# Gate and up multiplied together in a float32 decoder layer, two of eight chunk pairs by Strassen's seven products

## The chip, the cores and the metric

The kernel runs on one core of a Trainium2 chip. The metric is the device time of one execution in microseconds (us); lower is better. TensorE (PE) multiplies and transposes, VectorE (DVE) and ScalarE (ACT) work elementwise, GpSimd (POOL) does a few sums and issues DMAs, and SyncE (SP) issues most of the DMAs.

## The reference

A decoder layer on 256 tokens of width 2048, all in float32: a SwiGLU feed-forward, a mixer (attention and RWKV-7), cross-attention into a memory, a second feed-forward and a final norm. The change touches the two feed-forwards, the first loads and the last norm with its stores.

```python
D_MODEL = 2048
...
SEQ = 256
...
D_FF = 5632
...
def rms_norm(x, g):
    xf = x.astype(jnp.float32)
    y = xf * lax.rsqrt(jnp.mean(xf * xf, axis=-1, keepdims=True) + NORM_EPS)
    return (y * g.astype(jnp.float32)).astype(x.dtype)

def swiglu(h, w_gate, w_up, w_down):
    return (jax.nn.silu(h @ w_gate) * (h @ w_up)) @ w_down
...
        x = x + 0.5 * swiglu(rms_norm(x, ffn1_norm[l]), ffn1_w_gate[l], ffn1_w_up[l], ffn1_w_down[l])
...
        x = x + 0.5 * swiglu(rms_norm(x, ffn2_norm[l]), ffn2_w_gate[l], ffn2_w_up[l], ffn2_w_down[l])
    return rms_norm(x, final_norm)
```

## The kernel before

**Products.** A float32 factor is kept as two parts, hi (rounded to the type float32r) and lo (what is left). One float32 product is three TensorE products that accumulate in PSUM: hi by hi, hi by lo, lo by hi (`multiply`, lines 336 to 338). The stationary operand is a 128x128 piece of the activations: 128 features of one chunk k, 128 tokens; the two halves of the 256 tokens are t = 0 and 1. The moving operand is 128 features by 512 columns of a weight, and the result is a PSUM bank of 128 tokens by 512 columns.

**Weights.** They come from HBM once, in the order of `plan`. A unit is two chunks (KU = 2, called a chunk pair here) by 512 columns. `load` issues its DMA on SP's queue; in the feed-forwards one load fetches two units, 1 MB, into one of four buffers `raw2` (elsewhere one unit into one of four buffers `raw`). `divide` splits a unit: ScalarE casts raw to hi (line 299), VectorE subtracts to get lo (line 300). There are three buffers of each, so a unit can be split when the third unit before it has been multiplied. `next_unit` loads up to eight units ahead and splits up to two ahead (AHEAD). A unit serves 12 products: two chunks, two token halves, three parts.

**A feed-forward.** `feed_forward` goes through eleven blocks j of 512 columns of the hidden layer, in groups of 4, 4 and 3. A block is two calls of `product`, each over eight units (KD = 16 chunks): gate, whose two banks ScalarE turns into silu (line 415), then up, whose two banks VectorE multiplies by the row scale r and the silu (line 418) into `hb`. The result is then transposed on TensorE in two steps of four and split into hi and lo (`transposed`, lines 347, 352 and 353); these steps are interleaved with the products of what follows. After a group come four products with the down weights.

**Order.** The program is written as one stream; `bg` (class Interleave) holds generators of side work, and each `bg.tick()` between products lets every group of them take a step. A scheduler then places each engine's instructions, and every engine runs its own queue in that fixed order, waiting on semaphores.

**PSUM** has eight banks: three `acc` for products, three `mm` for the mixer, two `tr` for transposes.

**Opening and end.** Line 239 fills the first norm's gain by way of TensorE. SP first loads the sinks, then x in two halves of its first 512 columns with 1 MB of gate weights after each (lines 456 to 461). In the second feed-forward POOL's queue reloads x and loads the final gain early (`reload`); at the end line 1183 stores each half of the tokens in four DMAs on SP's queue.

Of the kernel before, what the change touches and what calls it, by code (L numbers as in the profile page):

```python
# [15 lines left out]
P = 128  # L16
# [20 lines left out]
EDGES = (34, 71)  # L37
# [42 lines left out]
def feed_forward_plan(wg, wu, wd):  # L80
    for j0, nj in GROUPS:
        for j in range(j0, j0 + nj):
            for w in (wg, wu):
                yield w, 0, KD, j * 512, 512
        for n in range(4):
            yield wd, 4 * j0, 4 * nj, n * 512, 512


def weight_plan(a):

    w = {n: v[0] for n, v in a.items() if "_w_" in n or n.startswith("w_")}
    yield from feed_forward_plan(w["ffn1_w_gate"], w["ffn1_w_up"], w["ffn1_w_down"])
    w_in = w["w_in"]
# [21 lines left out]
    for n in range(4):  # L115
        yield w["w_cross_o"], 0, 4, n * 512, 512
    yield from feed_forward_plan(w["ffn2_w_gate"], w["ffn2_w_up"], w["ffn2_w_down"])
# [3 lines left out]
def decoder_layer(ctx: ExitStack, tc: tile.TileContext, a: dict, out: bass.AP):  # L121
# [41 lines left out]

    def select(out, in_, pattern, op, fill, base, mult):
# [40 lines left out]
    nc.sync.dma_start(sinks[:], a["attn_sinks"].broadcast_to([P, 16]))  # L205
# [62 lines left out]
    plan = list(weight_plan(a))  # L268
    units = [(w, k0 + k, c0, n) for w, k0, nk, c0, n in plan for k in range(0, nk, KU)]
    raws, parts = {}, {}  # L270
    at = {"unit": 0, "product": 0, "pool": None}
    ends = [sum(nk // KU for _, _, nk, _, _ in plan[:i]) for i in (EDGES[0], EDGES[1])]

    def load(u):
# [10 lines left out]
        for i in range(m):  # L285
            raws[u + i] = raw[:, i * KU : (i + 1) * KU, :]
        nc.sync.dma_start(
            raw[:], w[k * P : (k + m * KU) * P, c0 : c0 + n].rearrange("(a p) n -> p a n", p=P)
        )

    def divide(u):
        if u >= len(units) or u in parts:
            return
# [3 lines left out]
        for s in (slice(0, 1), slice(1, 2)) if u == 0 else (slice(0, KU),):  # L297
# [3 lines left out]
        parts[u] = hi, lo  # L301

    def next_unit():
        u = at["unit"]
        at["unit"] += 1
        for v in range(u, u + (2 * LOADED if at["pool"] is not None else LOADED)):
            load(v)
            if v <= u + AHEAD:
                divide(v)
        return parts[u]  # L310

    def product(x: Act, w, skew=False):
# [6 lines left out]
        for k in range(0, nk - KU * len(skewed), KU):  # L319
            bg.until(lambda: all(k + i in x.done for i in range(KU)))  # L320
            u = next_unit()
# [3 lines left out]
        last = [(k, next_unit()) for k in skewed]  # L325
# [4 lines left out]

    def multiply(o, x, u, k, t, nk):
        hi, lo = u
        s = slice(t * P, (t + 1) * P)
        for i in range(KU):
            xh, xl = (x.at(p, k + i)[:, s] for p in range(2))
            pe.matmul(o, xh, hi[:, i, :], start=k + i == 0, stop=False)  # L336
            pe.matmul(o, xh, lo[:, i, :], start=False, stop=False)  # L337
            pe.matmul(o, xl, hi[:, i, :], start=False, stop=k + i == nk - 1)  # L338
# [60 lines left out]
    def feed_forward(sp, x, norm: Norm, wg, wu, wd, done, last=False):  # L399
        for gi, (j0, nj) in enumerate(GROUPS):  # L400
# [10 lines left out]
            for j in range(j0, j0 + nj):  # L411
                pg = product(norm.x, wg)
                hb = sp.tile([P, 2, 512], F32, tag="hb", name="hb", bufs=3)
# [7 lines left out]
                bg.spawn("feat", transposed(hb, 4 * (j - j0)))  # L421
            for n in range(4):
# [24 lines left out]
    with tc.tile_pool(name="f1", bufs=1, reuse_waits="tile") as sp:  # L447
# [695 lines left out]
    with tc.tile_pool(name="f2", bufs=1, reuse_waits="tile") as sp:  # L1143
# [3 lines left out]
        fin = sp.tile([P, D], F32, name="fin")  # L1147

        def reload():
            for n in range(4):  # L1150
# [3 lines left out]
                yield from idle(4)  # L1154
                pool.dma_start(
                    fin[:, cb], a["final_norm"][cb].unsqueeze(0).broadcast_to([P, 512])
                )
# [56 lines left out]
```

## Time and profile before

| | us |
|---|---|
| median of three timed runs | 2323.39 (2322.45 to 2326.1) |
| the profiled execution | 2329.57 |
| its span | 2327.9 |
| TensorE busy in the span | 2303.2 |
| VectorE busy | 1261.3 |
| ScalarE busy | 1078.0 |
| POOL busy | 130.9 |

Durations below are from the one profiled execution. The products of TensorE overlap, so that its busy time counts more than the time a product adds; the distance between starts is the better measure. The DMAs moved 432.71 MB, 185 GB/s over the span counting HBM's side.

### The profile page before, as it was taken

Reading aid. Unit: us, or ns where it says so; the run is one execution under the profiler, and the core shown is the slowest. Engines: PE = TensorE matmul, PEld = TensorE weight load, DVE = VectorE, ACT = ScalarE, POOL = GpSimd, SP = SyncE. Lnnn points to the kernel's source line nnn. Section 1 sums busy time; section 2 is a strip of 40 time slices with the busy share of each in tenths; the row PEclk is TensorE's granted clock in tenths of the full one; section 3 lists DMA queues with packets and bytes.
Section 4 is the critical chain, followed back from the end, with each engine's and each line's share of the span. In section 5 each row is a group of like instructions: output and inputs, shape, how many; then the busy total and the mean of one; then the engine's idle time right before and its main releaser. Section 6 shows DMA issues by size and latency. Waiting matters only on the chain.

```text
span 2327.9 us, 27346 instructions
## 1 busy us (share of the span) xinstructions
PE 2303.2 (99%) x10853; PEld 1893.5 (81%) x10853; DVE 1261.3 (54%) x1395; ACT 1078.0 (46%) x1425; POOL 130.9 (6%) x192
## 2 busy tenths in 40 slices
PE   8999999999999999999999999999999999999998
PEld 7888888888888877778888888888888888888886
DVE  4545544554556467886444466546545544554545
ACT  5443344434445468534434446455444344434444
POOL 1000000000000000200320030001000000000001
PEclk9999999999999999999999999999999999999999
DMA  8565655556554544677533576648555565556653
GB/s 291 182 196 184 198 187 193 186 193 197 183 193 151 170 129 135 198 214 212 151 85 96 158 259 217 201 154 298 192 188 191 190 197 183 197 183 197 192 188 127
DMA packets 219856, 432.71 MB, mean 186 GB/s; under 512 B 14267, under 2 KB 17040, under 8 KB 219728
## 3 DMA queue, kind: packets, MB, share of 16 engines
q1 hardware_dynamic: 211520, 405.58, 54.7%
q0 software_dynamic: 8176, 25.38, 3.4%
q8 instruction: 85, 1.39, 0.2%
q14 instruction: 43, 0.35, 0.0%
q10 hardware_dynamic: 32, 0.01, 0.0%
HBM read 417.56 MB, written 13.11 MB: 185 GB/s over the span
## 4 chain that ended last, share of the span: by engine, by line
PE 92%; issue 4%; DMA 2%; DVE 1%; ACT 1%; POOL 0%; SPq 0%; ACTq 0%; POOLq 0%; DVEq 0%
PE acc L336 28%; PE acc L337 28%; PE acc L338 28%; PE tr L347 2%; PE mm L924 1%; PE tr L893 1%; DVE lo L300 0%; PE mm L542 0%; DMA raw<-in_ffn_w_gate_dram 0%; DMA raw<-in_w_out_dram 0%; ACT hi L299 0%; PE tr L911 0%; DMA raw<-in_w_in_dram 0%; ACT s L567 0%; PE tr L994 0%
## 5 line engine op out<-in xcount | busy, mean ns | idle before, releaser
L300 DVE TENSOR_TENSOR lo<-raw,hi 128x1024 fp32r<-128x1024 f32 (+1 forms) x769 | 943.2, 1227 | 956.0 <-ACT hi L299 955.4
L299 ACT CAST hi<-raw 128x1024 fp32r<-128x1024 f32 (+1 forms) x769 | 805.4, 1048 | 1061.2 <-PE acc L338 1027.8
L336 PE MATMUL acc<-hi,xhi 128*128 128x512 f32 (+1 forms) x2016 | 799.5, 397 | 1.4 <-ACT hi L299 1.2
L337 PE MATMUL acc<-lo,xhi 128*128 128x512 f32 (+1 forms) x2016 | 787.2, 390 | 2.1 <-DVE lo L300 2.1
L338 PE MATMUL acc<-hi,xlo 128*128 128x512 f32 (+1 forms) x2016 | 785.9, 390 | 0.0
L336 PEld LDWEIGHTS acc<-hi,xhi 128*128 128x128 f32 x2016 | 380.3, 189 | 82.9 <-issue 5.4
L337 PEld LDWEIGHTS acc<-lo,xhi 128*128 128x128 f32 x2016 | 380.7, 189 | 81.1 <-DVE lo L300 3.3
L338 PEld LDWEIGHTS acc<-hi,xlo 128*128 128x128 f32 x2016 | 380.2, 189 | 79.2 <-issue 1.0
L336 PE MATMUL acc<-hi,hhi 128*128 128x512 f32 x704 | 275.5, 391 | 0.0
L338 PE MATMUL acc<-hi,hlo 128*128 128x512 f32 x704 | 274.2, 389 | 0.0
L337 PE MATMUL acc<-lo,hhi 128*128 128x512 f32 x704 | 274.0, 389 | 0.0
L338 PEld LDWEIGHTS acc<-hi,hlo 128*128 128x128 f32 x704 | 132.1, 188 | 27.8
L336 PEld LDWEIGHTS acc<-hi,hhi 128*128 128x128 f32 x704 | 132.2, 188 | 26.9
L337 PEld LDWEIGHTS acc<-lo,hhi 128*128 128x128 f32 x704 | 132.2, 188 | 26.9
L336 PE MATMUL acc<-hi,mthi 128*128 128x512 f32 x128 | 51.2, 400 | 0.0
L338 PE MATMUL acc<-hi,mtlo 128*128 128x512 f32 x128 | 50.1, 392 | 0.0
L337 PE MATMUL acc<-lo,mthi 128*128 128x512 f32 x128 | 49.9, 390 | 0.0
L1167 POOL TENSOR_TENSOR x<-x,fin 128x512 f32<-128x512 f32 x6 | 8.9, 1505 | 692.1 <-ACT junk L1165 692.1
L470 POOL DMA_DIRECT2D x1d<-x x4 | 3.0, 744 | 710.4 <-DVE x L427 710.4
L415 ACT ACTIVATE hb<-acc,rs 128x512 f32<-128x512 f32 x44 | 30.2, 690 | 19.5 <-PE acc L338 19.5
L352 ACT CAST hhi<-tr 128x512 fp32r<-128x512 f32 x44 | 25.7, 584 | 16.3 <-PE tr L347 16.3
L373 ACT ACTIVATE xhi<-tr,gains 128x256 fp32r<-128x256 f32 x48 | 22.0, 471 | 22.8 <-DVE xlo L374 16.1
(290 smaller groups left out, 1625.5 us busy)
## 6 DMA issues: line engine op xcount, KB each, us to landing
raw<-in_ffn_w_up_dram SPq DMA_DIRECT2D x88, 1024.0 KB, 5.2
raw<-in_ffn_w_down_dram SPq DMA_DIRECT2D x88, 1024.0 KB, 5.1
raw<-in_ffn_w_gate_dram SPq DMA_DIRECT2D x86, 1024.0 KB, 5.2
raw<-in_w_in_dram SPq DMA_DIRECT2D x136, 512.0 KB, 3.7
raw<-in_w_out_dram SPq DMA_DIRECT2D x32, 512.0 KB, 4.6
raw<-in_w_proj_attn_dram SPq DMA_DIRECT2D x16, 512.0 KB, 3.7
raw<-in_w_proj_rwkv_dram SPq DMA_DIRECT2D x16, 512.0 KB, 5.9
raw<-in_w_cross_kv_dram SPq DMA_DIRECT2D x16, 512.0 KB, 3.6
```

The source lines that it names most:

```text
L299: act.copy(hi[:, s], raw[:, s])
L300: dve.tensor_tensor(lo[:, s], raw[:, s], f32(hi[:, s]), ALU.subtract)
L336: pe.matmul(o, xh, hi[:, i, :], start=k + i == 0, stop=False)
L337: pe.matmul(o, xh, lo[:, i, :], start=False, stop=False)
L338: pe.matmul(o, xl, hi[:, i, :], start=False, stop=k + i == nk - 1)
L347: pe.transpose(b[:, o : o + P], tok[:, t, col : col + P], ident[:])
L352: act.copy(x.at(0, c, n), src)
L373: last = act.activation(self.x.at(0, c), b[:, j, :], AF.Copy, scale=g)
L415: act.activation(hb[:, t, :], pg[t][:], AF.Silu, scale=norm.r[t])
L893: pe.matmul(b[e][:, m * P : (m + 1) * P], x1[r, j, cs_], x2[r, j, cs_], start=True, stop=True,)
L924: pe.matmul(vb[:, o : o + P][:, r], lhs(e), rhs[:, r], start=first and e == 0, stop=True, **ek,)
L1167: pool.tensor_tensor(xs, xs, fin[:, n * 512 : (n + 1) * 512], ALU.mult)
```

## The change

Blocks j = 1 to 10 of each feed-forward multiply gate and up together (`product_pair`); j = 0 and the down products stay as they were. An item is then a unit of gate and the unit of up for the same chunks, and `next_item` loads and splits by items. For the chunk pairs 0, 2, 4, 5, 6 and 7 an item costs four times six products, as before. For pairs 1 and 3 (SEVEN) the two chunks, two token halves and two weights form a 2 by 2 times 2 by 2 product, which is done by Strassen's scheme in Winograd's form: seven products (each of three parts) in place of eight. `sums` makes the four combinations of the weights on VectorE and splits them; `combinations` makes those of the activations on POOL once per feed-forward. The seven products accumulate in seven banks p1 to p7 (three mm, two acc, two tr) over both pairs; after pair 3 VectorE adds p1, p6, p7 and p5 to what the other banks collect (`u2`, `u3`), and pair 0 (EARLY) uses differences of activations for p3, so that the sum comes out. After the last pair VectorE adds these to p2, p4, p3 and p5.

The opening gives TensorE nine products of ones, loads x by 512 columns and the first gate weights in smaller pieces, one of them on ScalarE's queue, and moves the sinks' load to POOL's queue. The final gain is loaded in the last group of the second feed-forward into two `raw` buffers. The last stores are three per half, on SP's and ScalarE's queues. `hb` has two buffers in place of three.

```diff
+SEVEN = (1, 3)
+EARLY = tuple(q for q in range(max(SEVEN)) if q not in SEVEN)
...
+            if j == 0:
+                for w in (wg, wu):
+                    yield w, 0, KD, j * 512, 512
+            else:
+                yield (wg, wu), 0, KD, j * 512, 512
...
+    idle_bank = mm()
+    for _ in range(9):
+        pe.matmul(idle_bank[:, :P], ones[:], ones[:], start=True, stop=True)
...
-    nc.sync.dma_start(sinks[:], a["attn_sinks"].broadcast_to([P, 16]))
+    pool.dma_start(sinks[:], a["attn_sinks"].broadcast_to([P, 16]))
...
+        for k in range(k0, k0 + nk, 2 * KU):
+            u = len(units)
+            units += [(v, k + i, c0, n) for v in w for i in (0, KU)]
+            items += [(u, u + 2), (u + 1, u + 3)]
...
+    def sums(g, u):
...
+        sp, rg, ru = at["pool"], raws[g], raws[u]
+        ta, tb = (wp.tile([P, KU, 512], F32, tag="raw", name="raw", bufs=4) for _ in range(2))
+        hi = sp.tile([P, 4, 512], F32R, tag="thi", name="thi")
+        lo = sp.tile([P, 4, 512], F32R, tag="tlo", name="tlo")
+        dve.tensor_tensor(ta[:, 0], ru[:, 0], rg[:, 0], ALU.subtract)
+        dve.tensor_tensor(ta[:, 1], ru[:, 1], ru[:, 0], ALU.subtract)
+        dve.tensor_tensor(tb[:, 0], ru[:, 1], ta[:, 0], ALU.subtract)
+        dve.tensor_tensor(tb[:, 1], rg[:, 1], tb[:, 0], ALU.subtract)
+        for i, t in enumerate((ta, tb)):
+            act.copy(hi[:, 2 * i : 2 * i + 2], t[:])
+            dve.tensor_tensor(
+                lo[:, 2 * i : 2 * i + 2], t[:], f32(hi[:, 2 * i : 2 * i + 2]), ALU.subtract
+            )
+        return hi, lo
+
+    def divide(i):
...
+        g, u = items[i]
+        if units[g][1] // KU in SEVEN:
+            parts[i] = split_unit(g), split_unit(u, slice(1, 2)), sums(g, u)
+        else:
+            parts[i] = split_unit(g), split_unit(u)
+
+    def next_item():
+        i = at["item"]
+        at["item"] += 1
+        u = items[i][0]
         for v in range(u, u + (2 * LOADED if at["pool"] is not None else LOADED)):
             load(v)
...
+        divide(i)
+        room = AHEAD
+        for j in range(i + 1, min(i + 1 + AHEAD, len(items))):
+            room -= len(items[j])
+            if room < 0:
+                break
+            for v in items[j]:
+                load(v)
+            divide(j)
+        return parts[i]
...
+    def combinations(sp, x: Act):
...
+            for q in range(max(SEVEN) + 1):
+                while not {2 * q, 2 * q + 1} <= x.done:
+                    yield
...
+                pool.tensor_tensor(
+                    v[:].rearrange("p k t n -> p k (t n)"), f32(x.at(0, 2 * q, 2)),
+                    f32(x.at(1, 2 * q, 2)), ALU.add,
+                )
+                if q in SEVEN:
+                    n = 4
+                    pool.tensor_tensor(f[:, 0], v[:, 0, 1], v[:, 1, 1], ALU.add)
+                    pool.tensor_tensor(f[:, 1], f[:, 0], v[:, 0, 0], ALU.subtract)
+                    pool.tensor_tensor(f[:, 2], v[:, 0, 0], v[:, 0, 1], ALU.subtract)
+                    pool.tensor_tensor(f[:, 3], v[:, 1, 0], f[:, 1], ALU.subtract)
+                else:
+                    n = 2
+                    pool.tensor_tensor(f[:, :2], v[:, :, 0], v[:, :, 1], ALU.subtract)
+                yield from idle(3)
+                s = slice(o, o + n)
+                act.copy(parts[0][:, s], f[:, :n])
+                dve.tensor_tensor(parts[1][:, s], f[:, :n], f32(parts[0][:, s]), ALU.subtract)
...
+    def product_pair(sp, x: Act, c, r, w):
...
+        def add(to, x_, w_, last):
+            if to not in b:
+                b[to] = {"p1": mm, "p3": mm, "p5": mm, "p2": acc, "p4": acc}.get(to, tr)()
+            times(
+                b[to][:], x_, w_, to not in begun, last, skip_group_check=True,
+            )
...
+                seven = (
+                    ("p1", of_x(0, k), of_w(g, 0), end), ("p2", of_x(0, k + 1), of_w(g, 1), False),
+                    ("p3", of_c(q, 3), of_w(u, 1), False), ("p5", of_c(q, 0), of_w(s, 0), end),
+                    ("p7", of_c(q, 2), of_w(s, 1), end), ("p6", of_c(q, 1), of_w(s, 2), end),
+                    ("p4", of_x(1, k + 1), of_w(s, 3), False),
+                )
+                for i, p in enumerate(seven):
+                    add(*p)
+                    if i % 2:
+                        bg.tick()
+                    if end and i == 1:
+                        act.copy(hb[:, 0], b["p1"][:])
+                if end:
+                    dve.tensor_tensor(u2[:], b["p6"][:], hb[:, 0], ALU.add)
+                    dve.tensor_tensor(u3[:], b["p7"][:], u2[:], ALU.add)
+                    dve.tensor_tensor(u2[:], b["p5"][:], u2[:], ALU.add)
+                continue
+            g, u = next_item()
+            for to, t, wt in (("p2", 0, g), ("p4", 1, g), ("p3", 0, u), ("p5", 1, u)):
+                for i in range(KU):
+                    off = to == "p3" and q in EARLY
+                    add(
+                        to, of_c(q, i) if off else of_x(t, k + i), of_w(wt, i),
+                        last and i == KU - 1,
+                    )
+                if last:
+                    if to == "p2":
+                        dve.tensor_tensor(hb[:, 0], b["p2"][:], hb[:, 0], ALU.add)
+                        act.activation(hb[:, 0], hb[:, 0], AF.Silu, scale=r[0])
+                    elif to == "p4":
+                        dve.tensor_tensor(hb[:, 1], b["p4"][:], u3[:], ALU.add)
+                        act.activation(hb[:, 1], hb[:, 1], AF.Silu, scale=r[1])
+                    else:
+                        t, v = (0, u2) if to == "p3" else (1, u3)
+                        dve.tensor_tensor(v[:], b[to][:], v[:], ALU.add)
+                        dve.scalar_tensor_tensor(
+                            hb[:, t], v[:], r[t], hb[:, t], ALU.mult, ALU.mult
+                        )
...
-        for c in (slice(0, 256), slice(256, 512)):
-            nc.sync.dma_start(x[:, :, c], W["x"][:, c].rearrange("(t p) n -> p t n", p=P))
-            load(c.start // 256)
-        for n in range(1, 4):
+        nc.sync.dma_start(col(0), blk(W["x"], 0))
+        load(0, ((slice(0, 1), act), (slice(1, 2), nc.sync), (slice(2, 4), nc.sync)))
+        nc.sync.dma_start(col(1), blk(W["x"], 1))
+        load(2, ((slice(0, 2), nc.sync), (slice(2, 4), nc.sync)))
+        for n in range(2, 4):
             nc.sync.dma_start(col(n), blk(W["x"], n))
-            load(n + 1)
+            load(2 * n)
...
+        def gain():
+            for n in range(4):
+                if n % 2 == 0:
+                    fins.append(wp.tile([P, KU, 512], F32, tag="raw", name="raw", bufs=4))
+                cb = slice(n * 512, (n + 1) * 512)
+                pool.dma_start(fin(n), a["final_norm"][cb].unsqueeze(0).broadcast_to([P, 512]))
+                yield
...
-                nc.sync.dma_start(out[0, t * P : (t + 1) * P, cb], xs)
+            for cb, queue in ((slice(0, 1024), nc.sync), (slice(1024, 1536), act),
+                              (slice(1536, 2048), nc.sync)):
+                queue.dma_start(out[0, t * P : (t + 1) * P, cb], x[:, t, cb])
```

In the built program the line numbers of the changed kernel are: the split 324 and 325, the sums 335 to 338 with their split 340 and 341, the three products 397 to 399, the block's first additions 499 to 501, its last steps 513 to 521.

More of the change, by code (lines that the diff above doesn't have):

```diff
@@ L286, in load, with split_unit @@
             raws[u + i] = raw[:, i * KU : (i + 1) * KU, :]
[L287 to L293, printed above, removed]
+        for i, queue in pieces or ((slice(0, m * KU), nc.sync),):
+            rows = slice((k + i.start) * P, (k + i.stop) * P)
+            queue.dma_start(raw[:, i], w[rows, c0 : c0 + n].rearrange("(a p) n -> p a n", p=P))
+    def split_unit(u, rows=slice(0, KU)):
         n, raw = units[u][3], raws[u]
@@ L324, in product @@
                 bg.tick()
-        last = [(k, next_unit()) for k in skewed]
+        last = [(k, next_item()) for k in skewed]
         for t in range(2):
@@ L329, in product, with times @@
         return o
+    def times(o, x, w, first, last, **how):
+        (xh, xl), (hi, lo) = x, w
+        pe.matmul(o, xh, hi, start=first, stop=False, **how)
+        pe.matmul(o, xh, lo, start=False, stop=False, **how)
+        pe.matmul(o, xl, hi, start=False, stop=last, **how)
     def multiply(o, x, u, k, t, nk):
-        hi, lo = u
         s = slice(t * P, (t + 1) * P)
         for i in range(KU):
[L335 to L338, printed above, removed]
+            times(
+                o, [x.at(p, k + i)[:, s] for p in range(2)], [w[:, i, :] for w in u],
+                k + i == 0, k + i == nk - 1,
+            )
```

105 lines of the change are left out of this document (78 added, 27 removed).

## The prediction

> **What bounds the kernel now.** I read the page's busy times, its chain of waits and its costliest groups first, then the timeline, first of VectorE and then of TensorE, over one feed-forward block.
>
> ```profile
> span 2327.9 us, 27346 instructions
> PE 2303.2 (99%) x10853; PEld 1893.5 (81%) x10853; DVE 1261.3 (54%) x1395; ACT 1078.0 (46%) x1425; POOL 130.9 (6%) x192
> ...
> PE 92%; issue 4%; DMA 2%; DVE 1%; ACT 1%; POOL 0%; SPq 0%; ACTq 0%; POOLq 0%; DVEq 0%
> ...
> L300 DVE TENSOR_TENSOR lo<-raw,hi 128x1024 fp32r<-128x1024 f32 (+1 forms) x769 | 943.2, 1227 | 956.0 <-ACT hi L299 955.4
> L299 ACT CAST hi<-raw 128x1024 fp32r<-128x1024 f32 (+1 forms) x769 | 805.4, 1048 | 1061.2 <-PE acc L338 1027.8
> L338 PE MATMUL acc<-hi,xlo 128*128 128x512 f32 (+1 forms) x2016 | 785.9, 390 | 0.0
> ...
> raw<-in_ffn_w_up_dram SPq DMA_DIRECT2D x88, 1024.0 KB, 5.2
> ```
>
> TensorE is busy for 99% of the span and makes up 92% of the chain that ended last. But the 390 ns of one product is not its price, since products overlap. VectorE's timeline gives the pace: each of its splits waits for a weight buffer that TensorE has just released, once per unit of 12 products.
>
> ```profile
> 188.14 1.23 DVE L300 TENSOR_TENSOR lo<-raw,hi 128x1024 fp32r<-128x1024 f32 x1 [1.49 <-ACT hi L299]
> 190.86 1.23 DVE L300 TENSOR_TENSOR lo<-raw,hi 128x1024 fp32r<-128x1024 f32 x1 [1.49 <-ACT hi L299]
> 192.00 1.40 DVE L418 SCALAR_TENSOR_TENSOR hb<-acc,rs,hb 128x512 f32<-128x512 f32 x2
> 193.59 1.23 DVE L300 TENSOR_TENSOR lo<-raw,hi 128x1024 fp32r<-128x1024 f32 x1 [0.18 <-ACT hi L299]
> ```
>
> Two splits start 2.72 us apart, so a product costs 2.72 / 12 = 0.227 us. A block of gate and up (j) is 16 units, 43.5 us; the same split starts at 149.10 and at 193.59, so the whole period is 44.5 us, of which 1.0 are the transposes of the block before and their surroundings. In that period VectorE has 16 splits and little else and waits some 1.49 us in every unit. The rows also show that a VectorE operation whose inputs are ready starts about 0.09 us before the one ahead of it ends (190.86 + 1.23 = 192.09, next start 192.00). So TensorE's issue is the bound, and VectorE and ScalarE, at 54% and 46%, have room.
>
> **The change, part by part.**
>
> *Strassen.* Twenty blocks (j = 1 to 10 in both feed-forwards) change. In each, chunk pairs 1 and 3 take 7 x 3 = 21 products in place of 24: 6 products fewer per block, 120 in all. The built order has 3 x 3040 products of 512 columns on TensorE before and 3 x 3000 after, so this is really done. Worth 120 x 0.227 = **27.2 us**. Order of products and banks change: three products per bank in place of six. No row has runs of three, but the change of bank after every sixth product costs nothing (starts stay 0.227 apart across it); I take 0.
>
> *VectorE, per changed block.* Removed: one half of two splits. Added per seven: four 128x512 subtractions and two 128x1024 splits; per block three sums of products and four additions. From the built order a pair block that is followed by another holds 18 operations of 1.23 (row L300), 19 of 0.69 (128x512; rows L353 and L427 of the costliest groups have 688 and 683 ns) and 2 of 0.74 (L418): 36.8 us, or 33.4 with the 0.09 overlap. The new period is 186 x 0.227 + 1.0 = 43.1 us. So VectorE goes from half busy to some 80%, and what matters is where its queue is dense. ScalarE gets about 23 of 43 us and stays under.
>
> I walked the built VectorE queue through such a block, time 0 at the first product, using: a buffer is free 0.19 us after the last product's slot ends, ScalarE casts for 1.05, VectorE starts 0.04 later. Chunk pair 4 begins at 21.4, 5 at 26.8, 6 at 32.2, 7 at 37.7, the next block at 43.1. Until the split of pair 6's up weights (30.8 to 32.0) VectorE waits for buffers in every unit, so nothing is late. From there it is packed:
>
> | VectorE, in queue order | starts | ends |
> |---|---|---|
> | three sums for the next block's pair 1 | 31.9 | 33.8 |
> | split gate 7, fourth sum, split of sums | 33.7 | 36.7 |
> | split up 7, second split of sums, split next gate 0 | 36.6 | 40.2 |
> | p2 and p4 tails (L513, L516) | 40.1 | 41.4 |
> | split next up 0 (its cast ends at 41.64) | 41.7 | 42.9 |
> | p3, p5 tails (p5 ends at 43.3) | 42.8 | 44.1 |
> | two products with r (L521) | 44.0 | 44.8 and 45.4 |
>
> TensorE's next block has the first transpose after 8 products, at 44.9, and the second two products later, at 45.4; in the queue behind them stands every further product. So the two results come just in time: slack about 0. The sums wait, besides, for a 1 MB load of up weights that is issued when the split of up 5 ends (26.6); with the median of 5.2 us (the load row above) it lands at 31.8, 0.1 before it is needed. Bounds of the stall: 0 if the overlap holds; without the overlap the 16 operations from 31.9 come about 1.0 us later. I take 0.25 for the 14 places where a pair follows a pair, and 0.1 for the 6 where the down product follows (no sums for a next block there): **4.1 us** lost, bounds 0 and 14 x 1.05 + 6 x 0.3 = 16.5. Sums for pair 3 fall where VectorE waits 1 to 2 us per unit; cover: the units of pairs 2 and 3.
>
> *Transposes* of a block's result stay 8 per block:
>
> ```profile
> 150.77 0.40 PE L338 MATMUL acc<-hi,xlo 128*128 128x512 f32 x1
> ...
> 151.01 0.60 PE L347 MATMUL tr<-ident,hb 128*128 128x128 f32 x4
> ...
> 151.37 0.48 PE L336 MATMUL acc<-hi,xhi 128*128 128x512 f32 x1
> ```
>
> Products around the four transposes start 0.60 apart in place of 0.23, as before; no change.
>
> *The opening.* Today the first product waits for a whole 1 MB of gate weights:
>
> ```profile
> 7.43 0.62 ACT L299 CAST hi<-raw 128x512 fp32r<-128x512 f32 x1 [3.26 <-DMA raw<-in_ffn_w_gate_dram]
> ...
> 8.99 0.78 PE L336 MATMUL acc<-hi,xhi 128*128 128x512 f32 x1
> ...
> 9.57 0.63 PE L337 MATMUL acc<-lo,xhi 128*128 128x512 f32 x1
> ...
> 9.99 0.63 PE L336 MATMUL acc<-hi,xhi 128*128 128x512 f32 x1
> ```
>
> ```profile
> 35.47 1.28 ACT L415 ACT_TABLE_LOAD   x1 [0.35 <-PE acc L338]
> ```
>
> The starts are 0.42 apart until about 13.8 us and 0.23 after 14.6: twelve products lose 0.2 each, 2.4 us; the clock column reads 1.00 throughout. The gate product ends at 35.5. After the change 256 KB of gate weights and 512 KB of x come first; at the 369 GB/s of the stretch from 4 to 8 us that brings the cast from 7.43 to about 6.1, 1.3 us. Nine idle products from about 1.0 us on may take away part of the 2.4. Against this stand 4 new casts on ScalarE (1.9 us), which is busy 3.4 of every 4 us from 16 to 28, each waiting for sums on POOL, whose queue first issues its DMAs (until 13.1 before, half a microsecond later now, since the sinks' load moved to it). I take **+1.5 us**, bounds -2.5 and +4. [...]
>
> POOL's sums also touch VectorE:
>
> ```profile
> 2288.43 2.97 POOL L1167 TENSOR_TENSOR x<-x,fin 128x512 f32<-128x512 f32 x2 [13.35 <-ACT junk L1165]
> ...
> 2290.49 2.00 DVE L300 TENSOR_TENSOR lo<-raw,hi 128x1024 fp32r<-128x1024 f32 x1 [1.50 <-ACT hi L299]
> ```
>
> A split beside a POOL addition took 2.00 in place of 1.23, so 0.77 each. In the second feed-forward the 1.49 us of waiting per unit hides it; in the opening up to four long POOL additions could cost 3 us. [...]
>
> *The end.* Four output DMAs become three per half, on two queues.
>
> ```profile
> 2322.27 0.75 DVE L1178 SCALAR_TENSOR_TENSOR x<-x,rs,fin 128x512 f32<-128x512 f32 x1
> 2322.38 1.80 SPq L1183 DMA_DIRECT2D out_dram<-x  x4
> ```
>
> The last operation ends at 2323.0, the fourth issue at 2324.2; with two issues on SP and one on the other queue the last starts at about 2323.2 against 2323.8. **0.6 us** gained, bounds 0 and 1.2. The final gain's loads move from POOL's queue at the second feed-forward's start to its last group; six units of 2.72 us pass before the first use, longer than the 9.6 us landing of those loads: 0.
>
> Sum: 27.2 - 4.1 + 1.5 + 0.6 = 25.2 us. The profiled execution took 2329.57 us, its span 2327.9; these become 2304.4 and 2302.7. The median of the three timed runs is 6.2 below the profiled one; the same difference taken from it gives **2298 us**.
>
> **Rivals.**
> 1. *The packed stretch is a microsecond too long.* For: 16 operations with next to no wait, slack 0. Against: the 0.09 overlap shows wherever two operations meet. 27.2 - 16.5 + 2.1 = 12.8: 2311 us.
> 2. *The loads become the bound; slower.* The load of the next up weights is issued only after up 5's split. If it lands after 9.5 us, as the gate load issued at 3.29 did in the opening (9.49 in the chain), the sums and all behind them are 4.3 - 0.4 late, with 0.25 that is 4.1 x 14 = 58 us: 2323 + 58 - 29 = 2352 us. It decides from 29 / 14 = 2.1 us of stall, a landing of 7.7. Against: 5.2 is the median of 88, and the loads before and after it are 5 us away; engines of the DMA are 60% busy.
> [...]
> 4. *Nothing is won*, because the idle before TensorE's products grows as much as they shrink; this needs 1.5 us of stall in all 20 blocks: 2323 us.
>
> **How the numbers follow.** Forecast 0.55, rival 1 0.20, rival 3 0.12, rival 2 0.08, rival 4 0.05. A measurement tells apart 0.2%, 4.6 us. Forecast, 1 and 3 are all faster: 0.87; same 0.05; slower 0.08. The forecast's own bounds are 27.2 + 4 + 1.2 = 32.4 (2291) and 27.2 - 16.5 - 2.5 = 8.2 (2315); the range 2290 to 2314 takes in rivals 1 and 3 and leaves out 2 and 4.
>
> **What would show it.** The count and pace of the products: 0.227 apart, period 43.1 in pair blocks. The transposes of a pair's result: idle on TensorE before them of 0 to 0.3 us with VectorE's L521 as releaser is the forecast, about 1 us is rival 1. The sums (L335) waiting for the load of up weights show rival 2. First product near 7.6 us and the gate product's end near 34 show the opening. If VectorE idles long in pairs 5 to 7, or the products' pace is not 0.227, my walk is wrong.

## The result and the profile after

The changed kernel takes 2309.62 us (median of four runs, 2306.61 to 2312.1). Four runs of the kernel before on the same chip have a median of 2324.72 us (2322.45 to 2326.1). The ratio is 0.9937, with a 95% interval from 0.9924 to 0.9949: 12 to 18 us faster, 15.1 by the medians. The predicted 2298 us is too low by 11.6, and inside the stated range of 2290 to 2314. The profiled execution of the changed kernel took 2307.24 us.

The page of the changed kernel, with the lines that answer to those shown of before (busy times, the chain of waits by engine, the costliest group of VectorE):

```profile
span 2305.5 us, 27706 instructions
PE 2279.0 (99%) x10751; PEld 1867.7 (81%) x10751; DVE 1511.0 (66%) x1784; ACT 1143.8 (50%) x1534; POOL 159.1 (7%) x221
...
PE 90%; issue 4%; DVE 2%; ACT 1%; DMA 1%; POOL 1%; SPq 0%; POOLq 0%; ACTq 0%; DVEq 0%
...
L325 DVE TENSOR_TENSOR lo<-raw,hi 128x1024 fp32r<-128x1024 f32 (+1 forms) x770 | 918.3, 1198 | 652.3 <-ACT hi L324 648.4
```

TensorE is still the bound. VectorE has 250 us more to do, and VectorE and POOL have gained a share of the chain of waits. In the four VectorE rows below, of the changed kernel's timeline, the same split stands 43.17 us apart in two neighbouring pair blocks (101.10 and 144.27). The period was 44.5 before, and 43.1 was predicted.

```profile
101.10 1.23 DVE L325 TENSOR_TENSOR lo<-raw,hi 128x1024 fp32r<-128x1024 f32 x1 [0.30 <-ACT hi L324]
...
144.27 1.22 DVE L325 TENSOR_TENSOR lo<-raw,hi 128x1024 fp32r<-128x1024 f32 x1 [0.29 <-ACT hi L324]
145.41 1.28 DVE L520 TENSOR_TENSOR u<-mm,u 128x512 f32<-128x512 f32 x2
146.61 1.40 DVE L521 SCALAR_TENSOR_TENSOR hb<-u,rs,hb 128x512 f32<-128x512 f32 x2
```

So Strassen's products bring what they should. To see where the rest went, the span is cut at three ends that every trace has: the last addition of the first feed-forward's down product to x, the last addition to x ahead of the second feed-forward, and in the second feed-forward the addition of the down product to the third quarter of x's columns. The tail is what follows the third end. Block 0 (j = 0) ends with VectorE's product with r. Times in us, from VectorE's timeline; the last four columns are runs described below.

| stretch | before | changed | no Strassen | late casts | sums on VectorE | both |
|---|---|---|---|---|---|---|
| first feed-forward, with the opening | 747.8 | 735.2 | 746.2 | 734.4 | 733.2 | 733.1 |
| of it, until block 0 ends | 60.0 | 60.5 | 58.4 | 59.8 | 58.5 | 58.3 |
| middle (code unchanged) | 843.0 | 836.7 | 838.0 | 837.0 | 840.6 | 838.4 |
| second feed-forward | 713.0 | 709.6 | 713.0 | 701.6 | 703.2 | 700.1 |
| of it, until block 0 ends | 44.3 | 54.0 | 44.3 | 46.4 | 47.7 | 45.7 |
| tail of the final norm, stores | 24.1 | 24.0 | 24.0 | 24.1 | 24.0 | 24.0 |
| span | 2327.9 | 2305.5 | 2321.1 | 2297.1 | 2301.0 | 2295.6 |

Behind block 0, each feed-forward of the changed kernel is 13.1 us shorter than before, 26.2 in all. Block 0 of the first loses 0.5, and block 0 of the second loses 9.7 (44.3 to 54.0), the end gains 0.1: 26.2 - 0.5 - 9.7 + 0.1 = 16.1. The middle differs by 6.3, although its code is the same. The record of the granted clock has 10.2 us at half speed there in the profiled execution of before (two dips) and none in that of after, which is worth about 5.1 by the products that half speed delays; the other 1.2 stays open. The timed runs give 15.1, near the 16.1 without the middle.

What happens in block 0 of the second feed-forward is seen on three engines. First ScalarE's timeline in the changed kernel:

```profile
1578.86 0.19 ACT L569 ACTIVATION_READ_ACCUMULATOR junk<-x 128x1 f32 x1
1583.33 0.40 ACT L438 CAST chi<-u 128x256 fp32r<-128x256 f32 x1 [4.28 <-POOL u L435]
1583.64 1.99 ACT L324 CAST hi<-raw 128x1024 fp32r<-128x1024 f32 x2
1590.02 0.62 ACT L438 CAST chi<-u 128x512 fp32r<-128x512 f32 x1 [4.39 <-POOL u L432]
1590.54 2.00 ACT L324 CAST hi<-raw 128x1024 fp32r<-128x1024 f32 x2
...
1599.01 0.62 ACT L438 CAST chi<-u 128x512 fp32r<-128x512 f32 x1 [3.98 <-POOL u L432]
```

The casts of the activation combinations (L438) wait 4.28, 4.39 and 3.98 us for POOL, and behind each of them in ScalarE's fixed queue stands a cast of weights (L324). In the run with the casts moved, below, the first two of these casts of weights start at 1578.40, which is 4.7 us earlier counted from the stage's start, so POOL was all that they waited for. POOL in the same stretch:

```profile
1573.00 1.33 POOL L423 TENSOR_TENSOR u<-xhi,xlo 128x512 f32<-128x512 f32 x1
1579.52 0.71 POOL L582 TENSOR_TENSOR rs<-ms,nhalf 128x2 f32<-128x2 f32 x1 [5.19 <-DVE ms L580]
1581.79 0.75 POOL L1360 DMA_DIRECT2D x<-x3d  x1 [1.55 <-issue]
1582.56 0.73 POOL L435 TENSOR_TENSOR u<-u 128x256 f32<-128x256 f32 x1
```

The first combination (L435) needs 0.73 us, but between the sum that feeds it (done at 1574.3) and itself stand the norm's power (L582), which waits 5.19 us for VectorE, and the issue of a reload of x. Then TensorE (rows of its timeline) and the stretch by windows (columns: length; busy time and instructions of PE, PEld, DVE, ACT, POOL; granted clock; DMA share and GB/s):

```profile
1582.29 0.39 PE L399 MATMUL acc<-hi,xlo 128*128 128x512 f32 x1
1584.73 0.73 PE L397 MATMUL acc<-hi,xhi 128*128 128x512 f32 x2 [2.06 <-ACT hi L324]
1586.75 0.80 PE L398 MATMUL acc<-lo,xhi 128*128 128x512 f32 x1 [1.29 <-DVE lo L325]
1587.34 0.63 PE L399 MATMUL acc<-hi,xlo 128*128 128x512 f32 x1
1587.77 0.63 PE L397 MATMUL acc<-hi,xhi 128*128 128x512 f32 x1
```

```profile
1576.00:1580.00 4.00, 4.00 (x19) 3.32 (x18) 1.99 (x6) 1.81 (x5) 0.48 (x1) 1.00 1.01 371
1580.00:1584.00 4.00, 2.67 (x12) 1.88 (x10) 0.24 (x1) 0.67 (x2) 2.40 (x5) 1.00 1.05 380
1584.00:1588.00 4.00, 1.98 (x5) 1.36 (x6) 4.00 (x3) 1.63 (x2) 3.98 (x4) 0.77 1.04 392
1588.00:1592.00 4.00, 4.00 (x15) 3.21 (x15) 1.42 (x3) 1.99 (x3) 3.25 (x5) 0.80 0.98 339
```

TensorE stops for 2.06 and 1.29 us, and then its products start 0.43 apart in place of 0.227, while the granted clock reads 0.77 and 0.80. A stop of 2.49 us, which ends at 1602.64, is followed by the same. The theory is thus: the casts that wait for POOL hold up the casts of weights, this stops TensorE, and part of the loss is the half rate behind the stop. The three stops make 5.84 us of the 9.7. A rival is that POOL's sums stretch VectorE's splits, as the prediction's row of 2.00 us showed (called the stretching from here on): two splits at 1591.83 took 2.89 us together, where two of 1.23 that follow each other, less the overlap, take about 2.37. Another rival is the clock alone.

### The profile page after: what moved, and what is told of

It is laid out like the page before. It is cut to its first block, busy times and chain, and to the rows that moved or that the text cites. A ratio compares the mean times of both kernels' runs of the same rounds, so it can differ in the third digit from the quotient of the medians.

```text
span 2305.5 us, 27706 instructions
## 1 busy us (share of the span) xinstructions
PE 2279.0 (99%) x10751; PEld 1867.7 (81%) x10751; DVE 1511.0 (66%) x1784; ACT 1143.8 (50%) x1534; POOL 159.1 (7%) x221
## 3 DMA queue, kind: packets, MB, share of 16 engines
q8 instruction: 84, 1.38, 0.2%
## 4 chain that ended last, share of the span: by engine, by line
PE 90%; issue 4%; DVE 2%; ACT 1%; DMA 1%; POOL 1%; SPq 0%; POOLq 0%; ACTq 0%; DVEq 0%
PE acc L397 21%; PE acc L398 21%; PE acc L399 21%; PE mm L399 6%; PE mm L397 6%; PE mm L398 6%; PE tr L534 2%; PE mm L1119 1%; PE tr L399 1%; PE tr L397 1%; PE tr L398 1%; DVE lo L325 1%; PE tr L1088 1%; ACT s L762 0%; ACT hi L324 0%
## 5 line engine op out<-in xcount | busy, mean ns | idle before, releaser
L324 ACT CAST hi<-raw 128x1024 fp32r<-128x1024 f32 (+1 forms) x770 | 784.4, 1025 | 930.1 <-PE acc L399 713.5
L397 PE MATMUL acc<-hi,xhi 128*128 128x512 f32 (+1 forms) x1256 | 500.1, 399 | 7.8 <-ACT hi L324 2.9
L398 PE MATMUL acc<-lo,xhi 128*128 128x512 f32 (+1 forms) x1256 | 491.6, 391 | 3.5 <-DVE lo L325 3.4
L399 PE MATMUL acc<-hi,xlo 128*128 128x512 f32 (+1 forms) x1256 | 490.3, 391 | 1.2 <-DVE xlo L561 1.2
L397 PEld LDWEIGHTS acc<-hi,xhi 128*128 128x128 f32 x1256 | 236.5, 188 | 60.6 <-issue 5.1
L398 PEld LDWEIGHTS acc<-lo,xhi 128*128 128x128 f32 x1256 | 237.0, 189 | 53.7 <-DVE lo L325 5.5
L399 PEld LDWEIGHTS acc<-hi,xlo 128*128 128x128 f32 x1256 | 236.5, 188 | 50.3 <-DVE xlo L561 2.5
L398 PE MATMUL mm<-lo,xhi 128*128 128x512 f32 x440 | 171.2, 389 | 0.0
L399 PE MATMUL mm<-hi,xlo 128*128 128x512 f32 x440 | 171.2, 389 | 0.0
L397 PE MATMUL mm<-hi,xhi 128*128 128x512 f32 x440 | 171.2, 389 | 0.0
L341 DVE TENSOR_TENSOR tlo<-raw,thi 128x1024 fp32r<-128x1024 f32 x80 | 95.9, 1219 | 19.9 <-ACT thi L340 19.9
```

The costliest lines, as they stand in the source:

```text
L324: act.copy(hi[:, s], raw[:, s])
L341: dve.tensor_tensor(lo[:, 2 * i : 2 * i + 2], t[:], f32(hi[:, 2 * i : 2 * i + 2]), ALU.subtract)
L397: pe.matmul(o, xh, hi, start=first, stop=False, **how)
L398: pe.matmul(o, xh, lo, start=False, stop=False, **how)
L399: pe.matmul(o, xl, hi, start=False, stop=last, **how)
```

## The experiments

The first four runs below were timed on one chip and the last four on another, each group beside the kernel before, whose medians were 2325.94 and 2325.32 us there and 2324.72 beside the changed kernel. A difference between runs of two groups is thus uncertain by about 1 us. The parts of a span come from one profiled execution each.

**The casts moved.** POOL's sums stay, ScalarE's casts of them go behind the silu of block 0.

```diff
-                yield from idle(3)
+                made.append((q, f, n))
+                yield
+            while c["after"] is None:
+                yield
+            for q, f, n in made:
                 s = slice(o, o + n)
-                act.copy(parts[0][:, s], f[:, :n])
+                with tc.issue_after(c["after"].ins):
+                    act.copy(parts[0][:, s], f[:, :n])
...
-                    act.activation(hb[:, t, :], pg[t][:], AF.Silu, scale=norm.r[t])
+                    c["after"] = act.activation(
+                        hb[:, t, :], pg[t][:], AF.Silu, scale=norm.r[t]
+                    )
```

> The changed kernel, but ScalarE's four casts of POOL's activation combinations stand behind the silu of block 0 in its queue, and not between the casts of the weights of block 0; POOL's sums are the same and stay where they were (their results lie in a buffer of their own until then). Theory A (the casts wait for POOL, ScalarE's weight casts queue behind them, TensorE stops and then runs at half rate): block 0 of the second feed-forward gets back most of the 9.7 us that it lost, block 0 of the first one 1 to 2 us, and the time falls from 2309.6 to about 2300 (2298 to 2303); ScalarE's waits for POOL of 4.3, 4.4 and 4.0 us are gone and the granted clock near 1590 and 1604 us is full. [...]

Measured: 2299.34 us (2298.36 to 2305.01), ratio to before 0.9893 (0.9880 to 0.9907), so 10.3 us below the changed kernel by the medians. Block 0 of the second feed-forward ends after 46.4 us in place of 54.0. Two rows of ScalarE's timeline in that block, and one of VectorE's:

```profile
1587.61 1.05 ACT L324 CAST hi<-raw 128x1024 fp32r<-128x1024 f32 x1 [1.66 <-PE acc L399]
1590.33 1.05 ACT L324 CAST hi<-raw 128x1024 fp32r<-128x1024 f32 x1 [1.67 <-PE acc L399]
```

```profile
1585.97 2.13 DVE L325 TENSOR_TENSOR lo<-raw,hi 128x1024 fp32r<-128x1024 f32 x1 [1.36 <-ACT hi L324]
```

The casts of weights wait for TensorE again, 2.72 us apart. A split beside POOL still takes 2.13 us in place of 1.23, and a POOL sum at 1586.99 takes 1.44 where the same kind took 0.46 elsewhere, so the two still stretch each other, but inside the waiting time of each unit. The granted clock is 1.00 in every window from 1572 to 1620, so the dips went together with the stops. So the stretching and the clock are not the main cause; the waiting casts are. The edit moves one thing more: POOL's four reloads of x now stand behind most of its sums (the first at 1591.31), which changes what the casts would have waited for and not that they no longer hold up the weights. The 2.1 us that block 0 still takes beyond the kernel without Strassen are not taken apart; in that time VectorE's sums of weights wait 3.62 us, until 1607.14, for a load of up weights.

**The sums on VectorE.** The casts stay where they were.

```diff
-                    pool.tensor_tensor(f[:, 0], v[:, 0, 1], v[:, 1, 1], ALU.add)
+                    dve.tensor_tensor(f[:, 0], v[:, 0, 1], v[:, 1, 1], ALU.add)
...
```

> The changed kernel with the sums of the activation combinations on VectorE in place of POOL; the casts stay where they were in ScalarE's queue. Theory A: VectorE makes each set of sums in 1 to 3 us where POOL took 4 to 8, so ScalarE waits some 1 us in place of 4 four times; of the 9.7 us some 7 to 9 come back: about 2301. [...] Rival C (the clock alone): 2309.6. Against all: VectorE gets about 2.5 us of sums per pair of activations in a block where it waits 1.5 us per unit, and could be late itself, which would show as TensorE waiting for the lo part in block 0: then 2305 or more.

Measured: 2304.0 us (2302.75 to 2306.03), ratio 0.9909 (0.9895 to 0.9923), three above what Theory A said. In the first feed-forward block 0 ends at 58.5, all that the combinations had cost. In the second it takes 47.7 us in place of 54.0, so 6.3 of the 9.7 come back and not the 7 to 9 of Theory A. The reason is near the case "against": VectorE's sums stand behind the norm's ms, which comes at 1580.96, and ahead of its splits, and the casts still stand ahead of the weights' casts. The window in which this falls, in this run:

```profile
1584.00:1588.00 4.00, 1.29 (x5) 0.43 (x3) 3.90 (x7) 3.68 (x5) 3.09 (x5) 1.00 1.03 386
```

TensorE is idle for 2.7 of 4 us here, in stops of 1.38 and 1.37 us, where the changed kernel had stops of 2.06, 1.29 and 2.49 us; and the granted clock stays at 1.00 in and behind it. The half rate does not follow every stop.

**No Strassen.** All chunk pairs take eight products; gate and up stay together, the new first and last DMAs too.

```diff
-SEVEN = (1, 3)
-EARLY = tuple(q for q in range(max(SEVEN)) if q not in SEVEN)
+SEVEN = ()
+EARLY = ()
...
```

> The changed kernel without Strassen's products: all chunk pairs take eight, and there are no sums of weights and no combinations of activations; gate and up are still multiplied together, and the first and last DMAs are the new ones. Theory A: it loses the 26.2 us of the fewer products and gets back the 9.7 us in the second feed-forward's block 0 and 1 to 2 in the first, so it is 15 to 16 slower than the changed kernel and 0 to 3 us faster than the kernel before: 2321 to 2325. The period of a block would be 44.5 us as before. If the pairing itself cost or won something (order of products and banks), the period in pair blocks would differ from 44.5 by that twentieth: 10 us in all would be 0.5 us per block.

Measured: 2323.77 us (2321.42 to 2326.48), ratio 0.9989 (0.9981 to 0.9998): 0.5 to 4.4 us faster than before. The second feed-forward takes 713.0 us, as before to the last digit, so multiplying gate and up together costs and wins nothing. Block 0 of the first ends at 58.4, 1.6 us earlier than before: that is the new opening without the combinations.

**A longer tail.** The fourth sum of weights for chunk pair 1 is made three times, 1.2 us more for VectorE in the packed stretch.

```diff
-        dve.tensor_tensor(tb[:, 1], rg[:, 1], tb[:, 0], ALU.subtract)
+        for _ in range(3 if units[g][1] // KU == SEVEN[0] else 1):
+            dve.tensor_tensor(tb[:, 1], rg[:, 1], tb[:, 0], ALU.subtract)
```

> The changed kernel with the fourth sum of weights of chunk pair 1 made three times (the same result), so that the packed stretch of VectorE's queue at a block's end is 1.2 us longer in the 14 places where a pair block follows a pair block (20 blocks have the sums; in the first of each group they lie elsewhere). Theory (slack next to nothing, as in the walk of the prediction): each of these places stops TensorE by 0.9 to 1.2 us more before the transposes, and if the stop is short the array keeps its rate: 13 to 17 us slower than the changed kernel, about 2324; the waits of TensorE for the products with r rise from 0.23 us each to above 1. Rival (the buffers ahead give the queue a microsecond or more of slack that the walk missed): within 3 us of 2309.6.

Measured: 2309.04 us (2307.57 to 2310.61), ratio 0.9929 (0.9916 to 0.9943), no slower than the changed kernel. The theory as I had put it falls. But the built order differs in another place as well. In just the 14 places the first transpose of a block's result stands behind 12 products of the next block and not behind 8, as in the changed kernel and still in the other 6. I take it that the scheduler reckoned with the later result and filled the time with products; the trace shows the order and not the reason. TensorE's timeline at the end of block 2 in this run:

```profile
148.12 0.39 PE L400 MATMUL acc<-hi,xlo 128*128 128x512 f32 x1
148.34 0.38 PE L535 MATMUL tr<-ident,hb 128*128 128x128 f32 x2
```

**The same with TensorE's order held.** From the ninth product of a block on, the products are tied behind the transposes, close to the changed kernel's order.

```diff
-        pe.matmul(o, xh, hi, start=first, stop=False, **how)
...
+        for i, (xs, ws) in enumerate(((xh, hi), (xh, lo), (xl, hi))):
+            n, trs = at.get("n", 99), at.get("trs", ())
+            at["n"] = n + 1
+            before = {8: 0, 9: 0, 10: 3, 11: 3}.get(n, 7 if n < 24 else 99)
+            with tc.issue_after(trs[before].ins) if 8 <= n and before < len(trs) else nullcontext():
+                pe.matmul(o, xs, ws, start=first and i == 0, stop=last and i == 2, **how)
```

> As the run with the fourth sum three times, but TensorE's order is held: the first transpose of a block's result stands behind 9 products of the next block, as in the changed kernel (8), where the planner had moved it behind 12. Theory (the slack of the tail is next to nothing, and the planner hid the 1.2 us by moving the transposes): the products with r end 0.83 us later, the transposes wait 0.5 to 0.8 us more in each of 14 places, 7 to 11 us in all over the run with the planner's order: 2316 to 2320. Rival (the tail has slack of its own): within 2 us of 2309.

Measured: 2317.66 us (2315.16 to 2318.74), ratio 0.9969 (0.9957 to 0.9981), 8.6 us above the run with the scheduler's order, 0.62 in each of the 14 places. The same place in this run:

```profile
148.15 0.39 PE L403 MATMUL acc<-hi,xhi 128*128 128x512 f32 x1
148.94 0.33 PE L540 MATMUL tr<-ident,hb 128*128 128x128 f32 x1 [0.41 <-DVE hb L526]
```

The distance from the product to the transpose, 0.22 us in the run above, is 0.79 here. In all, TensorE waits as follows for the products with r (total us, times, longest), a row that neither the run above nor the changed kernel has for PE:

```profile
PE tr L540 <- DVE hb L526: 7.5, 14, 1.7
```

That is most of the 8.6. The held order (first transpose behind 9 products) is not quite the changed kernel's, and no run has it without the longer tail, so the rest may be the order's. With that said, the tail has next to no slack of its own; the later place of the transposes gives it.

**The old opening.** First loads, sinks' queue and no idle products as in the kernel before, all else changed.

```diff
-        nc.sync.dma_start(col(0), blk(W["x"], 0))
-        load(0, ((slice(0, 1), act), (slice(1, 2), nc.sync), (slice(2, 4), nc.sync)))
...
+        for cc in (slice(0, 256), slice(256, 512)):
+            nc.sync.dma_start(x[:, :, cc], W["x"][:, cc].rearrange("(t p) n -> p t n", p=P))
+            load(cc.start // 256)
...
```

> The changed kernel with the first loads of the kernel before (x in two halves of 512 columns, 1 MB of gate weights after each, the sinks on SP's queue) and without the idle products. Theory: the opening is worth 1.6 us where nothing else is in the way (block 0 ended at 60.0 before and at 58.4 with the new opening and no combinations); with the combinations part of this is lost in ScalarE's waits for POOL, so 0.5 to 2 us slower than the changed kernel: 2310 to 2312, block 0 ending at 61 to 62.5. Rival (the new opening is itself what loses the time that the first block did not win): block 0 ends at or below 60.5, 2309 or less.

Measured: 2309.23 us (2308.66 to 2312.27), ratio 0.9936 (0.9924 to 0.9949). That is a little less than I expected, and the time alone can't tell it from the changed kernel. In the profile block 0 ends at 61.15 against 60.52, so the new opening keeps 0.6 of its 1.6 us once POOL and its casts are in the way, and it is not what loses time.

**Both cures together.** Sums on VectorE; in the second feed-forward sums and casts behind the silu of block 0.

```diff
+                while late and c["after"] is None:
+                    yield
+                lo = at.get("lo")
...
+                with tc.issue_after(lo.ins) if late else nullcontext():
+                    dve.tensor_tensor(
...
-        c = combinations(sp, norm.x)
+        c = combinations(sp, norm.x, last)
...
```

> The changed kernel with the sums of the activation combinations on VectorE; in the second feed-forward these sums and ScalarE's casts of them stand behind the silu of block 0, one set for every pair of chunks spread over the up product, where VectorE waits 1.5 us and ScalarE 1.67 us per unit. In the first feed-forward block 0 should end at 58.4 to 58.6 us as it did with the sums on VectorE (60.5 changed kernel, 59.8 late casts), and in the second the way from the last x update before it to the end of block 0 should take 44.3 to 45.5 us (54.0 changed kernel, 46.4 late casts, 47.7 VectorE sums, 44.3 with no sums at all). Time 2296 to 2299, 1 to 3 below the late casts. Against: sums of 5.6 us and their splits of 2.0 meet the sums of weights for block 1, so that the loads wait longer for buffers and come late, as one did in the run with the late casts (3.6 us of VectorE waiting for up weights): then no better than 2299.

Measured: 2298.62 us (2297.32 to 2300.38), ratio 0.9888 (0.9875 to 0.9902). Block 0 of the first feed-forward ends at 58.3. In the second it takes 45.7 us, a little over the range that I had given, but the whole second feed-forward takes 700.1, 12.9 below that without Strassen and near the 13.1 that the products are worth. From this kernel the changed one differs by 2.2 us in the first feed-forward and 9.5 in the second: that is the cost of where its combinations stand.

**No idle products.** The kernel just shown without them.

```diff
-    idle_bank = mm()
-    for _ in range(9):
-        pe.matmul(idle_bank[:, :P], ones[:], ones[:], start=True, stop=True)
```

> As the kernel of the run before (all sums on VectorE, late in the second feed-forward), without the nine idle products at the start. Theory: the first products then run at half rate, 0.42 apart, until about 12 us, but the third pair of transposes' x arrives only then (TensorE waited 1.0 us for it at 12.5 in the changed kernel, whose first products ran at full rate, and not at all in the kernels whose first products ran at half rate), so that the idle products buy 0 to 0.4 us. Rival (they win what the prediction's 2.4 us of slow products say, twelve products at 0.2 each): 1.5 to 2.4 us slower, and the half rate lasts beyond 12.5 us.

Measured: 2297.25 us (2295.63 to 2299.13), ratio 0.9882 (0.9869 to 0.9896), the fastest here and 12.4 us below the changed kernel by the medians; against the kernel with them, the intervals overlap. Block 0 ends at 58.38 against 58.34. TensorE in this run, and then in the kernel with both cures, which has the idle products:

```profile
9.34 0.63 PE L396 MATMUL acc<-hi,xlo 128*128 128x512 f32 x1
9.77 0.63 PE L395 MATMUL acc<-lo,xhi 128*128 128x512 f32 x1
...
12.52 0.50 PE L394 MATMUL acc<-hi,xhi 128*128 128x512 f32 x1
```

```profile
9.02 0.40 PE L398 MATMUL acc<-lo,xhi 128*128 128x512 f32 x1
9.26 0.39 PE L399 MATMUL acc<-hi,xlo 128*128 128x512 f32 x1
...
12.50 0.50 PE L397 MATMUL acc<-hi,xhi 128*128 128x512 f32 x1 [1.15 <-ACT xhi L565]
```

Without idle products the first ones start 0.43 apart, with them 0.23; but the next chunks' product starts at 12.5 in both, since it waits for the next columns of x. The faster start turns into a wait of 1.15 us.

## Why the prediction was right and wrong

*What bounds the kernel, and Strassen's worth: right.* 27.2 us were predicted for 120 products, and 26.2 came (13.1 in each feed-forward), at a distance of 0.227 us and a period of 43.17.

*The stall at the packed tail: mis-sized, 4.1 predicted and about 1.0 measured.* That is what lacks between 27.2 and 26.2, if all of it is put down to the tail. The waits view of the changed kernel:

```profile
PEld tr L534 <- DVE hb L521: 9.2, 40, 0.3
```

The 40 waits are of 0.2 to 0.3 us and on TensorE's weight loads, which partly run beside the products (81% and 99% of the span busy). The granted clock reads 1.00 from 60 to 735 us and from 1612 to 2240, where they lie, so waits this short cost no rate here. The walk of VectorE's queue was right to some tenths of a microsecond. Its slack of about 0 is borne out by the run with the order held. But what I took for a fixed order is not fixed: with 1.2 us more of VectorE's work that the scheduler knows of, the transposes stood four products later and the time was the same. So rival 1 (a packed stretch that is a microsecond too long) did not come about here, and would probably need a delay that the scheduler does not reckon with.

*Rivals 2 and 4: not here.* The sums (L335) waited 1.4 us in all for loads of up weights, and a period of 43.17 leaves no room for 1.5 us of stall in each block.

*The step that failed: POOL's sums in the second feed-forward, priced at 0* with "In the second feed-forward the 1.49 us of waiting per unit hides it". That sentence prices the stretched splits and is nearly right for them: the run with the casts moved has such splits too and loses at most 2.1 us there. It forgets the other half, which I had named for the opening alone: four casts that stand in ScalarE's queue ahead of casts of weights and wait for POOL. In the second feed-forward the waits are three times as long as in the opening (4.28 us against 1.18 and 1.39), because POOL's queue holds the norm's power and the reloads of x among the sums. That is read from its rows above; no run moves these two alone. Against 1.49 us per unit a wait of 4.3 us is not hidden. It cost 9.7 us, of which 7.6 came back with the casts moved. That the time still lies in the stated range is in part luck: the range was held open towards longer times for a stall at the tail that hardly came, and the 3.1 us by which that stall was priced too high made up for a third of this term. (The range ends at 2314; the bound of 8.2 us gained that it is taken from gives 2315.)

*The opening: +1.5 predicted, -0.5 measured.* The new loads are worth 1.6. The casts and POOL take 2.1 of it, which is within the bounds of -2.5 and +4 but on the other side. The signs named for the opening did not come: the first product starts at 8.01 and not near 7.6, and the table load behind the gate product starts at 35.98, against 35.47 before. That POOL's sums cost time by way of ScalarE's waits thus came about, but mainly in the second feed-forward (9.7 us lost in its block 0, against 2.1); I had reckoned with it for the opening alone, as rival 3, and gave it 0.12.

The clock column of 1.00 that the prediction read at the slow first products does not fit their spacing: in the run with the casts moved the window from 8 to 12 us has products 0.43 apart and a granted clock of 0.57, so this spacing is that of half speed.

That nine idle products may take away part of the 2.4 us was my estimate, and no run shows a gain from them (2298.62 us with them, 2297.25 without). The nine stand in the changed kernel's trace as 18 matmuls that took 4.21 us. With them the products started at full pace from the third on in the changed kernel (8.01, 8.37, 8.70, 8.94), but at half speed until about 12 us in the run with the casts moved, and 0.43 apart from 8.58 to 11.14 in the run with the order held. Either way it was worth nothing, since the next columns of x let TensorE go on only at 12.5.

*The end: 0.6 predicted, 0.1 measured.* The last issue does come earlier: 1.16 us behind VectorE's last operation before (2324.18 against 2323.02), 0.56 after (2301.25 against 2300.69). But the last stores took longer to land. The DMA view of the changed kernel's last 10 us (issues, KB each, median us to landing):

```profile
out_dram<-x SPq DMA_DIRECT2D x2, 512.0 KB, 2.7
out_dram<-x SPq DMA_DIRECT2D x2, 256.0 KB, 3.5
out_dram<-x ACTq DMA_DIRECT2D x2, 256.0 KB, 3.5
```

Before, eight stores of 256 KB on one queue had a median of 2.6. In these two traces the time gained at the issue is given back at the landing.

*The sum* by these terms: 25.2 - 9.7 (the failed step) - 2.0 (opening) - 0.5 (end) + 3.1 (Strassen with its stall: 26.2 in place of 23.1) = 16.1, against 15.1 timed.

## What to carry to other kernels

A cast or copy that waits for a slow engine costs what stands behind it in its own queue (here 7.6 us came back when four casts were moved); put side work behind the last urgent instruction of its stage, or on the engine that waits anyway. Price it by the wait for its producer, the producer's whole queue included, and not by its own duration (here 4.28 us of waiting against 0.40 of cast). Where a scheduler orders the work, a slack in its order is not a property of the kernel: hold the order before you measure it (here the two orders were 8.6 us apart).

## What the runs showed of the hardware

Between the opening and the tail of the final norm, the clock's records give half speed in pieces of 6.83 and 3.41 us in the kernel before and in two of 3.41 in the changed kernel; by the stops below, whether a stop of TensorE was followed by one is not settled by its length alone. In the traces of the changed kernel and of the three runs that kept POOL's sums and the early casts (longer tail, order held, old opening) there are 6.8 us of it in block 0 of the second feed-forward, where TensorE of the changed kernel stopped for 1.3 to 2.5 us at a time. The run with the sums on VectorE, with stops of 1.38 and 1.37 us there, had none. But at one same place in the middle, some 805 us into the span, where the code is unchanged and TensorE waits for a DMA, a stop of 1.54 us in the run with the sums on VectorE was followed by 3.41 us of half speed, and a stop of 1.97 us in the run with both cures by none. Each 3.41 us at half speed costs up to 1.7 us of products, so by this estimate up to 3.4 of the 9.7 us are an after-effect; with the 5.84 us of stops that is nearly all of it.

The same code in the middle took 836.7 to 843.0 us in the six traces of the table, and the two slowest are the ones with most time at half speed there (10.2 and 6.8 us). A difference of 5 us between two profiled executions need not come from the change.
